# First two expert pairs loaded by single row blocks, softmax and counts moved into the first product, and the last pairs' products in another order

## The chip, the cores and the metric

The kernel runs on one core of one Trainium2 chip. The metric is the time of one execution in device microseconds (us). Three runs of the kernel before took 1381.09, 1384.05 and 1386.32 us, a median of 1384.05.

## The reference, cut to what matters

One encoder layer over 256 tokens of 1024 channels in float32. A mixer (a gated DeltaNet and a gated short convolution) gives `x`, which the change leaves alone. Then come a normalisation, a router and a mixture of experts, in which nearly all of the change lies:

```python
logits = hf @ router_w + router_b                     # 256 tokens, 32 experts
top_val, top_idx = lax.top_k(logits, 4)
gates = softmax(top_val)
# for each expert, on the tokens that chose it:
gate, up = split(h @ w1[e] + b1[e])                   # w1[e]: 1024 x 2048
act = min(gate, 7) * sigmoid(1.702 * gate) * (clip(up, -7, 7) + 1)
y = act @ w2[e] + b2[e]                               # w2[e]: 1024 x 1024
x = x + gt_f * (sum over the 4 experts of gate * y)
return rmsnorm(x, final_norm_w)
```

The weights of one expert are 8 MB (w1) and 4 MB (w2), and all 32 experts are read.

## The kernel before

**Stages.** The mixer takes the first 425 us or so. Its weights come through the SP queue, and the first expert weights are loaded behind them. The rest is the experts.

**Pairs.** The experts are worked on in 16 pairs (`p` = 0 to 15). Two pairs make a quad (`q`), which shares one gathered input `xq` of 256 slots (8 groups of 32, dealt to the quad's four experts by `GROUPS`). Experts are sorted by how many tokens chose them, so the numbers of the experts from pair 2 on are read from `pidx_i` into registers of SP; pairs 0 and 1 are experts 0 to 3.

**A pair.** The first product (`first_product`, `w1_pair`) runs over eight row blocks `k` of w1, 128 rows each. A row block takes 16 matmuls of 128 x 512, which the trace shows as 32 records of line L1325 (`mm`). In front of it stand the biases (`w1_bias`, L120), and behind it the SwiGLU on VectorE and ScalarE (L1382 to L1386). `turn` (`to_ff`, transposes on L1328) turns the result into `aT`. The second product (`Second`, `block(c)`, four blocks of 32 records) multiplies it by w2. `end` scales its two halves (`scaled`, L1436) and hands back two calls of `combine`, which multiply by the gates and add to `x1` (L1429).

**Order.** The products go 0, 1, then second of 0, first of 2, second of 1, and so on: the second product of `p - 1` stands behind the first of `p`. While it runs in an odd `p`, the input of the next quad is gathered (`gather_part`, two `k` per call into one PSUM bank; the even one is evacuated by ScalarE on L1356, the odd one by VectorE on L1354). `mids`, a table by `k`, says what else is done behind a row block. TensorE's instructions of this stage are pinned, so that its order is the order of the program. Other engines' instructions are placed by a scheduler, which may bring them forward unless they are pinned. DMAs are issued by the queues of SP (weights) and ScalarE (small rows).

**Pair 0.** Its input is gathered with slots `P` that VectorE makes from the ranks `rk` (L1302, L1334), which come from a product on TensorE (L1297 to L1299). `route_counts` is traced behind the first product of pair 0: it copies the selection four times (L1500), counts, sorts, does the softmax (L1518 to L1524) and turns ranks and gates. `route_order` (in pair 1) reads its result.

**The ring of weights.** `RING` has nine slots of 2 MB. A slot is either one tile or two halves (the last two). `load_unit` (L982 for a whole slot, L986 for halves) puts two row blocks of one expert into a slot, as 256 rows of w1 or 512 half rows of w2: row `2p` and row `2p + 1` go to partition `p`. A slot is free when both row blocks have been consumed. Nine slots are filled in the mixer (`prefetch`, pinned): row blocks 0 to 5 of both experts of pair 0, and three slots of pair 1. Row blocks 6 and 7 of pair 0, 4 MB, go into working tiles that are not in use yet (L1316: `fw`, `pg`, `pgT`, two `aT`, two `g`, `u`, `th`, two `ysb`, `e4`).

**The end.** In pair 15 the second product of pair 14 stands inside the first product, behind `k` = 2 to 5, with its two combines behind `k` = 6. Then `to_ff` turns half of the result, and `w2_cols` does the second product by columns: 0 to 767 (two parts) and then 768 to 1023, each followed by its combines and by `finish_part` (squares on L1605, weighing with the final norm's weights on L1614). A branch for tokens over an expert's share (L1710) is not taken. Last come the sum of squares (L1778, L1779), the power -1/2 on POOL (`rsqrt`, L88), a scaling and the output.

Of the kernel before, what the change touches and what calls it, by code (L numbers as in the profile page):

```python
# [20 lines left out]
D = 1024  # L21
KT = D // 128
H = 8
NE = 32
# [29 lines left out]
def encoder_block(ctx, tc, x, c, ada_w, ada_b, norm1_w, w_in, conv_qkv_w, a_log, dt_bias, onorm_w,  # L54
# [79 lines left out]
    with ExitStack() as mix:  # L134
# [832 lines left out]
        def unit():  # L967
            tag = RING[unit_n[0] % len(RING)]
            first = unit_n[0] % len(RING) == RING.index(None)
            unit_n[0] += 1  # L970
            if tag:
                return (wk if tag == "hx" else wp_box[0]).tile([128, 4096], FT, name="wst", tag=tag, bufs=1), None
# [3 lines left out]
        def load_unit(src, fine=False, width=2048, hold=lambda i: i):  # L976
            t, halves = unit()
            r = src.shape[1] // 256
            if t is not None:
                halves = [t[:, 2048 * s:2048 * s + 2048] for s in range(2)]  # L980
            if t is not None and not fine:
                hold(nc.sync.dma_start(t, src.rearrange("e (p r) n -> p (e r n)", r=2 * r)))  # L982
            else:
                v = src.rearrange("e (p s r) n -> s p (e r) n", s=2, r=r)
                for s in range(2):
                    hold(nc.sync.dma_start(halves[s][:, 0:width].rearrange("p (r n) -> p r n", r=r), v[s]))  # L986
            return halves

        def w1_unit(p, c, m, regs, hold=lambda i: i):
            src = (moe_w1[0, 2 * p + m:2 * p + m + 1] if p < 2 else moe_w1[0, ds(regs[2 * (p % 2) + m], 1)])  # L990
            halves = load_unit(src[:, 256 * c:256 * c + 256, :], p == 2 * NQ - 1, hold=hold)
            return [[h[:, 512 * i:512 * i + 512] for i in range(4)] for h in halves]
# [3 lines left out]
        def w1_load(p, k, regs):  # L996
            if k % 2 == 0:
                w = pre.pop((p, k // 2), []) if p < 2 else []
                for m in range(len(w), 2):
                    w.append(w1_unit(p, k // 2, m, regs))  # L1000
                held_w[0] = w
            return [h[k % 2] for h in held_w[0]]

        pieces = iter([(0, c, m) for c in range(3) for m in range(2)] + [(1, 0, 0), (1, 0, 1), (1, 1, 0)])
        owed = [0]

        def prefetch(n=1):
            owed[0] += n
            for _, (p, c, m) in zip(range(owed[0] // 4), pieces):
                pre.setdefault((p, c), []).append(w1_unit(p, c, m, None, pin))  # L1010
            owed[0] %= 4
# [298 lines left out]
    for k, m, ts in ((KT - 2, 0, [fw, spare("pg"), spare("pgT")]), (KT - 2, 1, [spare("aT", 1024), spare("aT", 1024)]),  # L1310
                     (KT - 1, 0, [spare("g"), spare("g"), spare("u"), spare("th")]),
                     (KT - 1, 1, [spare("ysb"), spare("ysb"), e4])):
        c, qs = 0, []
        for t in ts:
            n = t.shape[1]
            nc.sync.dma_start(t, moe_w1[0, m, 768 + k % 2:768 + k % 2 + 255:2, c:c + n])  # L1316
            qs += [t[:, o:o + 512] for o in range(0, n, 512)]
            c += n
        pre.setdefault((0, 3), [[], []])[m].append(qs)

# [22 lines left out]
    def gather_part(P, xq, ks):  # L1343
        p = misc()
        for kk, k in enumerate(ks):
            o = p[:, kk * QS:(kk + 1) * QS]
            n = 0
            for t in range(2):
                for hx in (h2h, h2l):
                    mm(o, hx[:, t, 256 * (k // 2) + k % 2:256 * (k // 2) + k % 2 + 255:2], P[:, t],  # L1350
                                  start=n == 0, stop=n == 3, skip_group_check=True)
                    n += 1
            if k % 2:
                V.tensor_scalar(xq[:, k], o, facp[:, k:k + 1], facp[:, 8 + k:9 + k], op0=OP.mult, op1=OP.add)  # L1354
            else:
                A.activation(xq[:, k], o, AF.Identity, scale=facp[:, k:k + 1], bias=facp[:, 8 + k:9 + k])  # L1356
# [56 lines left out]
    def to_ff(gs, aT=None, halves=(0, 1)):  # L1413
        if aT is None:
            aT = work.tile([128, KT, 128], FT, name="aT", tag="aT", bufs=2)
        for half in halves:
# [23 lines left out]
    class Second:  # L1440
# [21 lines left out]
    def w2_cols(p, parts, aT, gt, regs, mids={}):  # L1462
# [5 lines left out]
        for c1 in range(0, 4, nc_):  # L1468
            w = []
            for m in range(2):  # L1470
                src = w2_rows(p, m, regs)[:, 256 * c1:256 * c1 + 256 * nc_, c0:c0 + n]
                if n > 256:
                    w.append(load_unit(src, True, 2 * n))
                else:
                    t, halves = unit()
                    if t is not None:
                        halves = [t[:, 2048 * s:2048 * s + 2048] for s in range(2)]
# [5 lines left out]
            for c in range(nc_):  # L1483
# [7 lines left out]
                for f in mids.get(c1 + c, ()):  # L1491
                    f()
        for y, (o, no) in zip(ys, parts):
            combine([gt[:, pa]], [scaled(y, o, no)], o, no)
# [3 lines left out]
    def route_counts():  # L1498
        for t in range(2):
            pin(V.tensor_copy(sel4[:, t, 1:4], sel4[:, t, 0:1].to_broadcast([128, 3, NE])))  # L1500
        p = misc()
# [15 lines left out]
        for t in range(2):  # L1517
            V.tensor_scalar(nmx[:, t:t + 1], mx[t][:, 0:1], -1.0, None, op0=OP.mult)  # L1518
            A.activation(ex[:, t], lg[:, t, 0:NE], AF.Exp, bias=nmx[:, t:t + 1])
            pin(V.scalar_tensor_tensor(ex[:, t], ex[:, t], 1.0, sel[:, t], op0=OP.mult, op1=OP.mult,  # L1520
                                       accum_out=den[:, t:t + 1]))
        pin(V.reciprocal(den, den))
        for t in range(2):
            pin(V.tensor_scalar(gat[:, t], ex[:, t, None, :].to_broadcast([128, 4, NE]), den[:, t:t + 1], None,  # L1524
                                op0=OP.mult))
        p = misc()
        for t in range(2):
            tr(p[0:NE, t * 128:(t + 1) * 128], rk[:, t], ident)
            tr(p[:, (2 + t) * 128:(3 + t) * 128], gat[:, t].rearrange("p b e -> p (b e)"), ident)
        rT = work.tile([NE, 2, 128], FT, name="rT", tag="ysb", bufs=2)  # L1530
# [66 lines left out]
    ssf = moe.tile([128, 2, len(PARTS)], FT, name="ssf")  # L1597

    def square(t, i, eng="a"):
# [4 lines left out]
        if eng == "a":  # L1604
            A.activation(junk, xv, AF.Square, accum_out=o)  # L1605
        else:
            V.scalar_tensor_tensor(junk, xv, 1.0, xv, op0=OP.mult, op1=OP.mult, accum_out=o)  # L1607

    def finish_part(xf, i, engs="aa"):
        cs = slice(PARTS[i][0], PARTS[i][0] + PARTS[i][1])  # L1610
        for t in range(2):
            square(t, i, engs[t])
        for t in range(2):
            V.tensor_tensor(xf[:, t, cs], x1[:, t, cs], fw[:, cs], op=OP.mult)  # L1614

    def final_row(h):
# [5 lines left out]
        A.copy(fw[:, 512 * h:512 * h + 512], p)  # L1622
# [26 lines left out]
    for p in range(NP):  # L1649
        q, pa = divmod(p, 2)  # L1650
        at = {k: [] for k in range(KT)}
        for i, f in enumerate(sums.pop(p - 2, ())):
            at[i].append(f)
        if p == 1:
# [22 lines left out]
        if p == 0:  # L1677
            turned.extend(route_counts())
# [138 lines left out]
```

## Time and profile before

| what | before |
|---|---|
| median of three runs | 1384.05 us |
| the profiled execution, its own time | 1383.1 us |
| its span, first to last instruction | 1381.4 us |
| TensorE (PE) busy | 1268.9 us, 92% |
| VectorE (DVE), ScalarE (ACT), GpSimd (POOL) busy | 37%, 20%, 11% |
| read from HBM | 486.82 MB |
| granted clock of TensorE, mean | 0.985 |

Times in the trace are microseconds from the start of the span. A busy TensorE is not TensorE at its peak, since matmuls overlap and their ends are modelled. "Idle before" is the time that the engine stood still before an instruction, with what ended it. The granted clock is 1.00 at 2.4 GHz and 0.50 at 1.2 GHz, the two levels. The DMA share is the mean busy share of the core's 16 DMA engines, and can read slightly over 1.

### The profile page before, as it was taken

How to read it: one execution, taken by the hardware profiler on the slowest of the kernel's cores; microseconds unless marked ns; L12 is line 12 of the kernel's file. 1: busy time of each engine (PE TensorE's matmuls, PEld its weight loads, DVE VectorE, ACT ScalarE, POOL GpSimd, SP SyncE). 2: the span in 40 equal slices, each digit the busy share in tenths (PEclk: the TensorE clock that was granted, in tenths of full speed). 3: DMA queues.
4: the chain of work that ended last, by engine and by line, in shares of the span. 5: the costliest groups of instructions: out<-in, count | busy, mean ns of one | idle time of the engine just before them, and what ended most of it. 6: DMA issues, size and time to landing. Idle time of an engine off the chain costs nothing. (4 is left out here: it accounts for less than half of the span.)

```text
span 1381.4 us, 24052 instructions
## 1 busy us (share of the span) xinstructions
PE 1268.9 (92%) x10284; PEld 661.2 (48%) x10285; DVE 514.7 (37%) x1020; ACT 282.0 (20%) x546; POOL 150.9 (11%) x126
## 2 busy tenths in 40 slices
PE   6999997999999899999998998989899898898986
PEld 4988896999996333223333222322322232232222
DVE  3387879876673232123112212221221212211113
ACT  3455552553652010101001000000100000000001
POOL 4555684000000000000000000000000000000000
PEclk9999999999999899999999999999999999999999
DMA  9978977227796799999999999999999999999993
GB/s 337 306 234 275 334 237 233 70 92 261 246 397 247 313 411 387 419 428 425 423 425 427 425 427 425 424 427 426 426 425 426 427 424 426 423 427 423 421 407 128
DMA packets 112882, 492.65 MB, mean 357 GB/s; under 512 B 8703, under 2 KB 64384, under 8 KB 82562
## 3 DMA queue, kind: packets, MB, share of 16 engines
q1 hardware_dynamic: 108528, 485.94, 88.3%
q10 hardware_dynamic: 4241, 5.12, 1.1%
q8 instruction: 82, 1.34, 0.4%
q14 instruction: 31, 0.25, 0.0%
HBM read 486.82 MB, written 4.21 MB: 355 GB/s over the span
## 5 line engine op out<-in xcount | busy, mean ns | idle before, releaser
L1325 PE MATMUL acc<-wst,XT 128*32 128x512 f32 x4088 | 469.8, 599 | 11.8 <-DMA wst<-in_moe_w_dram 11.8
L1325 PEld LDWEIGHTS acc<-wst,XT 128*32 128x32 f32 x4088 | 129.6, 110 | 326.6 <-issue 304.9
L1325 PE MATMUL acc<-wst,aT 128*32 128x512 f32 (+1 forms) x2112 | 250.2, 588 | 37.6 <-DMA wst<-in_moe_w_dram 36.9
L1325 PEld LDWEIGHTS acc<-wst,aT 128*32 128x32 f32 x2112 | 67.6, 111 | 190.9 <-issue 127.7
L314 PE MATMUL mm<-hh,wl 128*128 128x256 f32 (+1 forms) x520 | 149.4, 288 | 2.2 <-POOL wl L264 1.3
L312 PE MATMUL mm<-hh,wh 128*128 128x256 f32 (+1 forms) x520 | 150.2, 289 | 0.3 <-DVE cacc L560 0.3
L313 PE MATMUL mm<-hh,wh 128*128 128x256 f32 (+1 forms) x520 | 149.4, 287 | 0.0
L263 ACT CAST wh<-raw 128x1024 fp32r<-128x1024 f32 (+1 forms) x89 | 91.9, 1039 | 93.6 <-PE mm L313 54.9
L88 POOL TENSOR_TENSOR rs<-ss,half_m 128x2 f32<-128x2 f32 x3 | 2.1, 702 | 941.0 <-DVE ss L1779 883.6
L312 PEld LDWEIGHTS mm<-hh,wh 128*128 128x128 f32 (+1 forms) x520 | 99.5, 191 | 9.7 <-issue 5.5
L314 PEld LDWEIGHTS mm<-hh,wl 128*128 128x128 f32 (+1 forms) x520 | 99.5, 191 | 6.2 <-issue 2.5
L313 PEld LDWEIGHTS mm<-hh,wh 128*128 128x128 f32 (+1 forms) x520 | 99.5, 191 | 0.9 <-issue 0.8
L264 POOL TENSOR_TENSOR wl<-raw,wh 128x1024 fp32r<-128x1024 f32 x36 | 88.0, 2451 | 71.4 <-ACT wh L263 61.8
L1383 ACT ACTIVATE th<-g 128x512 f32<-128x512 f32 x32 | 20.2, 630 | 357.6 <-DVE g L1382 296.2
L1429 DVE TENSOR_TENSOR x<-x,misc 128x512 f32<-128x512 f32 (+1 forms) x66 | 44.2, 671 | 126.1 <-PE misc L1325 126.1
L1382 DVE TENSOR_SCALAR g<-acc 128x512 f32<-128x512 f32 x32 | 22.0, 688 | 180.6 <-PE acc L1325 180.6
L1436 DVE TENSOR_TENSOR ysb<-acc,gtf 128x512 f32<-128x512 f32 (+1 forms) x33 | 22.2, 675 | 172.0 <-PE acc L1325 172.0
L264 DVE TENSOR_TENSOR wl<-raw,wh 128x1024 fp32r<-128x1024 f32 (+1 forms) x53 | 65.7, 1247 | 28.8 <-ACT wh L263 28.6
L1354 DVE TENSOR_SCALAR XT<-misc,fac 128x256 f32<-128x256 f32 x32 | 17.4, 544 | 140.4 <-PE misc L1325 140.4
L1325 PE MATMUL misc<-ysb,pgT 128*128 128x512 f32 (+1 forms) x132 | 63.9, 606 | 1.6 <-DVE ysb L1436 0.9
L1325 PE MATMUL misc<-P,h2h 128*128 128x256 f32 x128 | 40.5, 339 | 20.5 <-ACT XT L1356 18.4
L1325 PEld LDWEIGHTS misc<-P,h2h 128*128 128x128 f32 x128 | 25.1, 196 | 53.1 <-issue 28.3
(387 smaller groups left out, 1378.9 us busy)
## 6 DMA issues: line engine op xcount, KB each, us to landing
wst<-in_moe_w_dram SPq DMA_DIRECT2D x136, 2048.0 KB, 28.6
wst<-in_moe_w_dram SPq DMA_DIRECT2D x100, 1024.0 KB, 28.6
raw<-in_w_in_dram SPq DMA_DIRECT2D x36, 1024.0 KB, 7.5
raw<-in_ada_w_dram SPq DMA_DIRECT2D x24, 1024.0 KB, 8.3
wst<-in_moe_w_dram SPq DMA_DIRECT2D x8, 768.0 KB, 17.7
raw<-in_w_out_sc_dram SPq DMA_DIRECT2D x4, 1024.0 KB, 10.1
raw<-in_w_up_a_dram SPq DMA_DIRECT2D x4, 1024.0 KB, 5.0
raw<-in_w_o_dram SPq DMA_DIRECT2D x4, 1024.0 KB, 9.9
```

The source lines that it names most:

```text
L88: G.tensor_tensor(dst, src, half_m.to_broadcast([128, n]), op=OP.pow)
L263: a = A.copy(wh, src)
L264: b = (V if job.lo == "v" else G).tensor_tensor(wl, src, wh.bitcast(FT), op=OP.subtract)
L312: PE.matmul(ps, wh[:, k, :], ah[:, k, :], start=k == 0, stop=False, skip_group_check=True)
L313: PE.matmul(ps, wh[:, k, :], al[:, k, :], start=False, stop=False, skip_group_check=True)
L314: PE.matmul(ps, wl[:, k, :], ah[:, k, :], start=False, stop=k == KT - 1, skip_group_check=True)
L1325: return held[0](PE.matmul(*a, **kw))
L1354: V.tensor_scalar(xq[:, k], o, facp[:, k:k + 1], facp[:, 8 + k:9 + k], op0=OP.mult, op1=OP.add)
L1382: V.tensor_scalar(g[:n], g_ps[:n], 7.0, None, op0=OP.min)
L1383: A.activation(th[:n], g[:n], AF.Tanh, scale=0.851)
L1429: V.tensor_tensor(xv, xv, p[:, 0:n], op=OP.add)
L1436: V.tensor_tensor(y, ps[:, 0:n], gtf_box[0][:, c0:c0 + n], op=OP.mult)
```

## The change

1. A slot takes one row block of both experts (`load_rows`) in the first and second products of pairs 0 and 1, for row blocks 6 and 7 of pair 15, and in the second product of pair 14. Other loads stay as they were.
2. Nine slots are still filled ahead: row blocks 0 to 6 of pair 0, and 0 and 1 of pair 1. The working tiles hold row block 7 of pair 0 and row block 4 of pair 1.
3. `softmax`, pinned, is traced behind the first two gathers. `route_counts` stands behind row block 6 of pair 0 and the copies of the turned ranks and gates (`turned_gates`) behind row block 7.
4. `gather_part` does the matmuls of both `k`, then evacuates.
5. In pair 15 only blocks 0 and 1 of pair 14's second product stand inside (behind `k` = 4 and 5). Blocks 2 and 3 follow row block 7, then the turn of pair 15 in one piece, one combine, the first two parts of `w2_cols`, the other combine, and then the parts' combines, one of them behind the last part's matmuls.
6. The squares of the last columns come ahead of their weighing. The division by 1024 and the epsilon go into the final weights (times 32) and into a fourth column of the sums.

```diff
-        def unit():
+        def slot():
...
+        def load_rows(srcs, hold=lambda i: i):
+            _, halves = slot()
+            for h, src in zip(halves, srcs):
+                hold(nc.sync.dma_start(h, src))
+            return halves
...
+        def w1_rows(p, k, regs, hold=lambda i: i):
+            c = 256 * (k // 2) + k % 2
+            return [quarters(h) for h in load_rows(
+                [w1_src(p, m, regs)[:, c:c + 255:2].rearrange("e p n -> p (e n)") for m in range(2)], hold)]
...
         def w1_load(p, k, regs):
+            if p < 2 or p == 2 * NQ - 1 and k >= KT - 2:
+                return pre.pop((p, k), None) or w1_rows(p, k, regs)
             if k % 2 == 0:
-                w = pre.pop((p, k // 2), []) if p < 2 else []
-                for m in range(len(w), 2):
-                    w.append(w1_unit(p, k // 2, m, regs))
-                held_w[0] = w
-            return [h[k % 2] for h in held_w[0]]
-
-        pieces = iter([(0, c, m) for c in range(3) for m in range(2)] + [(1, 0, 0), (1, 0, 1), (1, 1, 0)])
+                c = 256 * (k // 2)
+                held_w[0] = [load_unit(w1_src(p, m, regs)[:, c:c + 256]) for m in range(2)]
+            return [quarters(h[k % 2]) for h in held_w[0]]
+
+        pieces = iter([(0, k) for k in range(KT - 1)] + [(1, 0), (1, 1)])
...
-    for k, m, ts in ((KT - 2, 0, [fw, spare("pg"), spare("pgT")]), (KT - 2, 1, [spare("aT", 1024), spare("aT", 1024)]),
-                     (KT - 1, 0, [spare("g"), spare("g"), spare("u"), spare("th")]),
-                     (KT - 1, 1, [spare("ysb"), spare("ysb"), e4])):
+    for p, k, m, ts in ((0, KT - 1, 0, [spare("g"), spare("g"), spare("u"), spare("th")]),
+                        (0, KT - 1, 1, [spare("ysb"), spare("ysb"), spare("pg"), spare("pgT")]),
+                        (1, 4, 0, [spare("aT", 1024), spare("aT", 1024)]), (1, 4, 1, [e4, fw])):
...
                     mm(o, hx[:, t, 256 * (k // 2) + k % 2:256 * (k // 2) + k % 2 + 255:2], P[:, t],
                                   start=n == 0, stop=n == 3, skip_group_check=True)
                     n += 1
+        for kk, k in enumerate(ks):
+            o = p[:, kk * QS:(kk + 1) * QS]
             if k % 2:
...
         def block(self, c):
-            if c % 2 == 0:
-                self.w = [load_unit(w2_rows(self.p, m, self.regs)[:, 256 * c:256 * c + 512], self.p == 2 * NQ - 2)
-                          for m in range(2)]
-            w = [h[c % 2].rearrange("p (i n) -> p i n", i=2) for h in self.w]
+            if self.p < 2 or self.p == 2 * NQ - 2:
+                w = load_rows([w2_rows(self.p, m, self.regs)[:, 512 * (c // 2):512 * (c // 2) + 512]
+                               .rearrange("e (p s r) n -> s p (e r n)", s=2, r=2)[c % 2] for m in range(2)])
+            else:
...
+    def softmax():
         for t in range(2):
             pin(V.tensor_copy(sel4[:, t, 1:4], sel4[:, t, 0:1].to_broadcast([128, 3, NE])))
+        for t in range(2):
+            pin(V.tensor_scalar(nmx[:, t:t + 1], mx[t][:, 0:1], -1.0, None, op0=OP.mult))
+            pin(A.activation(ex[:, t], lg[:, t, 0:NE], AF.Exp, bias=nmx[:, t:t + 1]))
...
     for k in range(2):
         gather_part(P0, xq, (k,))
+    softmax()
     busy(2)
...
+    ssf = moe.tile([128, 2, len(PARTS) + 1], FT, name="ssf")
+    G.memset(ssf[:, :, len(PARTS):], D * EPS)
...
-        A.copy(fw[:, 512 * h:512 * h + 512], p)
+        A.activation(fw[:, 512 * h:512 * h + 512], p, AF.Copy, scale=float(D) ** 0.5)
...
+        if p == 0:
+            at[KT - 2].append(lambda: turned.append(route_counts()))
+            at[KT - 1].append(lambda: turned.extend(turned_gates(turned.pop())))
...
-            at[2].append(lambda: box.append(second(p - 1)))
-            for c in range(4):
-                at[2 + c].append(lambda c=c: box[0].block(c))
-            at[5].append(lambda: box.extend(box[0].end()))
-            at[6] += [lambda h=h: box[1 + h]() for h in range(2)]
+            at[4].append(lambda: box.append(second(p - 1)))
+            for c in range(2):
+                at[4 + c].append(lambda c=c: box[0].block(c))
...
-    last = (to_ff(gs[NP - 1], None, (0,)), gts[NQ - 1], regs[NQ - 1])
-    w2_cols(NP - 1, PARTS[0:2], *last, {0: [lambda: to_ff(gs[NP - 1], last[0], (1,))]})
-    for i in range(2):
-        finish_part(xf, i)
-    w2_cols(NP - 1, PARTS[2:3], *last)
+    for c in range(2, 4):
+        box[0].block(c)
+    turn(NP - 1)
+    before = box[0].end()
+    before[0]()
+    last = (aTs[NP - 1], gts[NQ - 1], regs[NQ - 1])
+    most = w2_cols(NP - 1, PARTS[0:2], *last)
+    before[1]()
+    most[0]()
+    finish_part(xf, 0)
+    rest = w2_cols(NP - 1, PARTS[2:3], *last)
+    most[1]()
+    finish_part(xf, 1)
+    rest[0]()
...
-    finish_part(xf, len(PARTS) - 1, "av")
...
-    V.tensor_reduce(ss3, ssf, axis=mybir.AxisListType.X, op=OP.add)
-    V.tensor_scalar(ss3, ss3, 1.0 / D, EPS, op0=OP.mult, op1=OP.add)
+    square(0, len(PARTS) - 1)
+    square(1, len(PARTS) - 1, "v")
+    pin(V.tensor_reduce(ss3, ssf, axis=mybir.AxisListType.X, op=OP.add))
     rsqrt(rs3, ss3)
+    weigh(xf, len(PARTS) - 1, pin)
```

## Rows read from the trace of the kernel before

**Rows 1.** The page: busy tenths of TensorE and DMA in 40 slices of the span

```profile
PE   6999997999999899999998998989899898898986
...
DMA  9978977227796799999999999999999999999993
```

**Rows 2.** Busy table: stretch, PE, PEld, DVE, ACT, POOL busy, clock, DMA share, GB/s

```profile
439.00:444.00 5.00, 5.00 (x48) 1.75 (x44) 0.54 (x1) 0.28 (x1) 0.00 (x0) 1.00 0.29 63
...
473.00:488.00 15.00, 15.00 (x110) 5.13 (x114) 4.05 (x25) 0.63 (x2) 0.00 (x0) 0.79 0.39 120
...
540.00:548.00 8.00, 8.00 (x55) 2.35 (x57) 2.75 (x4) 0.00 (x0) 0.00 (x0) 1.00 0.75 265
548.00:1200.00 652.00, 601.74 (x4822) 193.80 (x4818) 139.82 (x298) 42.69 (x73) 0.00 (x0) 0.99 1.01 425
...
1338.00:1360.00 22.00, 20.22 (x170) 7.06 (x166) 8.88 (x14) 2.46 (x4) 0.00 (x0) 1.00 0.83 309
```

**Rows 3.** Timeline of SP's queue, 434 to 600: start, duration, line, loads issued

```profile
442.28 17.82 SPq L982 DMA_DIRECT2D wst<-in_moe_w_dram  x6
...
544.66 28.63 SPq L982 DMA_DIRECT2D wst<-in_moe_w_dram  x7
```

**Rows 4.** Timeline of VectorE, 426 to 436: start, duration, line, operation, idle before

```profile
430.75 0.19 DVE L1520 SCALAR_TENSOR_TENSOR ex<-ex,sel 128x32 f32<-128x32 f32 x1 [1.45 <-ACT ex L1519]
...
431.79 0.22 DVE L1302 SCALAR_TENSOR_TENSOR rk<-misc,sel 128x64 f32<-128x64 f32 x1
```

**Rows 5.** Timeline of TensorE, 415 to 600 (same columns)

```profile
429.18 0.39 PE L1299 MATMUL misc<-sel,tri_s 128*128 128x32 f32 x2
...
432.69 0.36 PE L1325 MATMUL misc<-P,h2h 128*128 128x256 f32 x1 [2.15 <-DVE P L1334]
...
462.06 4.89 PE L1325 MATMUL acc<-wst,XT 128*32 128x512 f32 x42
471.45 1.06 PE L1325 MATMUL misc<-sel,one_f 128*128 128x32 f32 x4 [4.50 <-DVE sel L1500]
...
474.12 2.09 PE L120 MATMUL acc<-b1c,tri_ul 32*128 32x512 f32 x8
476.14 8.62 PE L1325 MATMUL acc<-wst,XT 128*32 128x512 f32 x64
...
496.92 7.07 PE L1325 MATMUL acc<-wst,XT 128*32 128x512 f32 x64
...
513.46 0.28 PE L1325 MATMUL misc<-P,h2l 128*128 128x256 f32 x1
514.40 0.39 PE L1325 MATMUL misc<-P,h2h 128*128 128x256 f32 x1 [0.66 <-ACT XT L1356]
```

**Rows 6.** DMA totals of 450 to 470 (2 MB loads), then 1290 to 1300 (1 MB loads)

```profile
DMA packets 588, 8.59 MB, mean 429 GB/s; under 512 B 64, under 2 KB 64, under 8 KB 64
...
DMA packets 578, 4.21 MB, mean 421 GB/s; under 512 B 64, under 2 KB 64, under 8 KB 64
```

**Rows 7.** Timeline of TensorE, 1262 to 1376

```profile
1282.60 1.24 PE L1328 MATMUL misc<-ident,g 128*128 128x128 f32 x8
...
1326.51 4.52 PE L1325 MATMUL acc<-wst,aT 128*32 128x512 f32 x25 [4.02 <-DMA wst<-in_moe_w_dram]
...
1341.68 3.89 PE L1325 MATMUL misc<-ysb,pgT 128*128 128x512 f32 x8
...
1355.07 7.95 PE L1325 MATMUL acc<-wst,aT 128*32 128x512 f32 x96
...
1367.26 3.66 PE L1325 MATMUL acc<-wst,aT 128*32 128x256 f32 x64
```

**Rows 8.** Timeline of VectorE, 1370 to 1377

```profile
1372.20 0.85 DVE L1429 TENSOR_TENSOR x<-x,misc 128x256 f32<-128x256 f32 x2 [0.79 <-PE misc L1325]
...
1374.47 0.15 DVE L1778 TENSOR_REDUCE ss<-ssf 128x2 f32<-128x6 f32 x1
1374.65 0.17 DVE L1779 TENSOR_SCALAR ss<-ss 128x2 f32<-128x2 f32 x1
```

More of the change, by code (lines that the diff above doesn't have):

```diff
@@ L971, in unit, with load_unit @@
             if tag:
-                return (wk if tag == "hx" else wp_box[0]).tile([128, 4096], FT, name="wst", tag=tag, bufs=1), None
+                t = (wk if tag == "hx" else wp_box[0]).tile([128, 4096], FT, name="wst", tag=tag, bufs=1)
+                return t, [t[:, 2048 * s:2048 * s + 2048] for s in range(2)]
             return None, [wp_box[0].tile([128, 2048], FT, name="wst", tag="s8", bufs=1) if first and s == 0 else
                           raw_tile([128, 2048], FT, "wst") for s in range(2)]
-        def load_unit(src, fine=False, width=2048, hold=lambda i: i):
-            t, halves = unit()
+        def load_unit(src, width=2048, fine=False):
+            t, halves = slot()
             r = src.shape[1] // 256
-            if t is not None:
-                halves = [t[:, 2048 * s:2048 * s + 2048] for s in range(2)]
             if t is not None and not fine:
-                hold(nc.sync.dma_start(t, src.rearrange("e (p r) n -> p (e r n)", r=2 * r)))
+                nc.sync.dma_start(t, src.rearrange("e (p r) n -> p (e r n)", r=2 * r))
             else:
@@ L1008, in prefetch @@
             owed[0] += n
-            for _, (p, c, m) in zip(range(owed[0] // 4), pieces):
-                pre.setdefault((p, c), []).append(w1_unit(p, c, m, None, pin))
+            for _, (p, k) in zip(range(owed[0] // 4), pieces):
+                pre[p, k] = w1_rows(p, k, None, pin)
             owed[0] %= 4
@@ L1309, in encoder_block @@
     e4 = dp.tile([128, 1024], FT, name="wst", tag="e4")
-    for k, m, ts in ((KT - 2, 0, [fw, spare("pg"), spare("pgT")]), (KT - 2, 1, [spare("aT", 1024), spare("aT", 1024)]),
-                     (KT - 1, 0, [spare("g"), spare("g"), spare("u"), spare("th")]),
-                     (KT - 1, 1, [spare("ysb"), spare("ysb"), e4])):
-        c, qs = 0, []
+    for p, k, m, ts in ((0, KT - 1, 0, [spare("g"), spare("g"), spare("u"), spare("th")]),
+                        (0, KT - 1, 1, [spare("ysb"), spare("ysb"), spare("pg"), spare("pgT")]),
+                        (1, 4, 0, [spare("aT", 1024), spare("aT", 1024)]), (1, 4, 1, [e4, fw])):
+        o, qs = 0, []
+        c = 256 * (k // 2) + k % 2
         for t in ts:
             n = t.shape[1]
[L1316 to L1319, printed above, removed]
+            nc.sync.dma_start(t, moe_w1[0, 2 * p + m, c:c + 255:2, o:o + n])
+            qs += [t[:, i:i + 512] for i in range(0, n, 512)]
+            o += n
+        pre.setdefault((p, k), []).append(qs)
     held = [pin]
@@ L1411, in w1_pair, with to_ff @@
         return [swiglu(128, pss[half], pss[2 + half]) for half in range(2)]
[L1413 to L1416, printed above, removed]
+    def to_ff(gs):
+        aT = work.tile([128, KT, 128], FT, name="aT", tag="aT", bufs=2)
+        for half in range(2):
             ps = misc()
@@ L1472, in w2_cols @@
                 if n > 256:
-                    w.append(load_unit(src, True, 2 * n))
+                    w.append(load_unit(src, 2 * n, True))
                 else:
-                    t, halves = unit()
-                    if t is not None:
-                        halves = [t[:, 2048 * s:2048 * s + 2048] for s in range(2)]
+                    _, halves = slot()
                     for h in range(2):
@@ L1490, in w2_cols, with route_counts @@
                                           tile_position=(0, 32 * j), skip_group_check=True)
[L1491 to L1494, printed above, removed]
+        return [lambda o=o, no=no, y=scaled(y, o, no): combine([gt[:, pa]], [y], o, no) for y, (o, no) in zip(ys, parts)]
     gtf_box = []
-    def route_counts():
+    def softmax():
         for t in range(2):
             pin(V.tensor_copy(sel4[:, t, 1:4], sel4[:, t, 0:1].to_broadcast([128, 3, NE])))
+        for t in range(2):
+            pin(V.tensor_scalar(nmx[:, t:t + 1], mx[t][:, 0:1], -1.0, None, op0=OP.mult))
+            pin(A.activation(ex[:, t], lg[:, t, 0:NE], AF.Exp, bias=nmx[:, t:t + 1]))
+        for t in range(2):
+            pin(V.scalar_tensor_tensor(ex[:, t], ex[:, t], 1.0, sel[:, t], op0=OP.mult, op1=OP.mult,
+                                       accum_out=den[:, t:t + 1]))
+        pin(V.reciprocal(den, den))
+        for t in range(2):
+            pin(V.tensor_scalar(gat[:, t], ex[:, t, None, :].to_broadcast([128, 4, NE]), den[:, t:t + 1], None,
+                                op0=OP.mult))
+    def route_counts():
         p = misc()
@@ L1516, in route_counts @@
         V.tensor_scalar(perm, tgt.rearrange("p q m -> p (q m)"), key[:, 1:2], None, op0=OP.is_equal)
[L1517 to L1525, printed above, removed]
         p = misc()
@@ L1529, in route_counts, with turned_gates @@
             tr(p[:, (2 + t) * 128:(3 + t) * 128], gat[:, t].rearrange("p b e -> p (b e)"), ident)
+        return p
+    def turned_gates(p):
         rT = work.tile([NE, 2, 128], FT, name="rT", tag="ysb", bufs=2)
```

29 lines of the change are left out of this document (16 added, 13 removed).

## The prediction

> **What bounds the kernel now.** I read the page's slices first. From about the fourteenth slice on, DMA and TensorE both read 9 or nearly so [rows 1], so the page alone does not say which one sets the pace. The busy table of chosen stretches does: from 548 to 1200 us the DMA share is 1.01 at 425 GB/s [rows 2]. DMA never rests there, while TensorE has 50 of 652 us idle. The second half is therefore bound by the weights' bytes, and a microsecond that DMA loses earlier comes out at the end.
>
> The same table shows where it loses time. At 425 GB/s the stretch 439 to 444 (63 GB/s) lost 5 x (1 - 63/425) = 4.3 us, 473 to 488 lost 10.8 us and 540 to 548 lost 3.0 us: 18.1 us together [rows 2]. The queue that issues the loads says why. Six loads start at 442.28 and seven at 544.66 [rows 3], each right after a pair of row blocks has been consumed: DMA had nothing to load into. TensorE sets those moments, so up to 548 TensorE is the bound, and after it DMA.
>
> Third comes TensorE's own order in that stretch [rows 4, 5]. It waits 4.50 us for the selection copies at 471.45, between the first products of pairs 0 and 1, and afterwards 64 records of row blocks take 8.62 us where a later 64 take 7.07 [rows 5]: the granted clock of 473 to 488 is 0.79 [rows 2].
>
> **Part 1: softmax behind the slots.** VectorE runs the softmax (from 430.75) ahead of the ranks at 431.79, from which P is made [rows 4]. The ranks' TensorE operand ended at 429.18 + 0.39 = 429.57 [rows 5]. With the softmax traced and pinned behind the gather, ranks and P move up by 431.79 - 429.63 (a handover of 0.06 by estimate) = 2.1 us, and pair 0 with them. The softmax itself, under 2 us of VectorE and ScalarE, then lies beside row blocks during which VectorE is nearly idle (0.54 of the 5 us from 439 [rows 2]); without that cover it would cost those 2 us again, and the second gather's evacuation queues behind it at worst.
>
> **Part 2: counts inside pair 0.** Now TensorE ends pair 0 at 462.06 + 4.89 = 466.95, idles, does counts and turns from 471.45, biases, then two row blocks that end at 476.14 + 8.62 = 484.76 [rows 5]. After the change the sequence is 466.95, plus counts and turns (471.45 to 474.12, or 2.67 at the lower clock, so 1.3 at the upper, by estimate), plus biases 1.1 (half of 2.09 and a handover), plus two row blocks 7.1: 476.5. That is 8.3 us earlier. VectorE's count chain and ScalarE's two copies are now queued ahead of the SwiGLU of pair 0, and the third and fourth bias of pair 1 wait for two of its reads; the row block of 3.5 us covers them. Uncovered, the bound is the old 4.5 us wait with its clock loss, so this term lies between 0 and 8.3.
>
> **Part 3: gather evacuated after both halves.** In pair 1's second product the second four gather matmuls start at 514.40, 0.94 us after the fourth began (513.46), where neighbours follow at 0.12 [rows 5]. Writing both halves of the bank before reading either saves 0.8 us, four times: 3.3 us. In later pairs it saves as much, but there TensorE has slack and it buys nothing.
>
> Together TensorE reaches the end of pair 2's second row block 2.1 + 8.3 + 3.3 = **13.7 us** earlier.
>
> **Part 4: single row blocks in the ring.** A 2 MB slot now holds one row block of both experts and is free after one row block, where two slots came free after two. At 425 GB/s a slot takes 4.9 us. Walk DMA on: the spares' loads end near 439.4; row 0 has freed a slot at 436, so the 439 hole goes. Seven slots come free inside pair 0 (six before), and keep DMA busy to 439.4 + 9 x 4.9 = 483.5 once pair 1's first two rows free theirs at 473 and 476.5; so the 473 hole goes. Eighteen slots in all last to 528. The next one waits for pair 2's second row block, in the old run 544.66 and now 544.66 - 13.7 = 531. A hole of 3 us stays, and DMA runs on without rest from there, 13.7 us ahead. So DMA's own bound is 18.1, TensorE's 13.7, and **the smaller counts**. After that, which slot holds what is as before. The queue issues two loads for one, at 0.3 to 0.4 us each against 4.9 us per slot, so that costs nothing unless issue takes over 2.4 us.
>
> Size of a load: 2 MB loads stream at 429 GB/s, 1 MB loads at 421 [rows 6]. Thirteen slots of row loads, 27.3 MB, come after 439 us; on these that is 1.2 us, inside the hole that stays. I take 0; the far end is the 309 GB/s of the slowest loads [rows 2], among the rivals.
>
> The Trainium skill, "DMA: Bandwidth & Descriptors" (Bandwidth, Measured), speaks against smaller loads: it gives 341 GB/s for one of 1 MB and 425 for 16 MB. By that, an estimate, the 27.3 MB would cost 16 us more and the end would come near 1375. The trace disagrees: with loads queued behind one another, 421 [rows 6].
>
> **Part 5: the tail.** Before, TensorE waited last for weights at 1326.51 [rows 7]; five more 1 MB blocks of these experts land by 1326.5 + 5 x 2.46 = 1338.8. Then it still had row blocks, two combines (3.89), row block 7 at 1345.50, an exposed SwiGLU, and the last second product, whose last add ended at 1373.05 [rows 7, 8].
>
> New order, on the same scale: the last landing is pair 14's fourth block, 1338.8. It takes 3.5, half of 7.07 (1342.3), pair 15's turn 1.2, one combine 1.9 (1345.4), two blocks of the last product at 7.95/3 = 2.65 each (1350.7) [rows 5, 7]. SwiGLU lies beside pair 14's blocks. The third block needs the seventh of eight loads of 256 x 768 floats, 0.79 MB each: at 309/0.83 = 372 GB/s [rows 2] 14 us or so after 1338.8, so 1352.8, a wait of 2.1. Two blocks to 1358.1, two combines 3.8 (1361.9), the last 64 records 3.66 (1365.6), then as now 2.1 to the last add: 1367.7. Gain 1373.05 - 1367.7 = **5.3 us**. With no wait it would be 7.4. If the waits for single blocks (some 1.5 us each at pair 14's third and fourth) bring the lower clock, it is 0 or less. I take 5.3: TensorE's wait of 2.15 us at 432.69 [rows 5] is nearest to these, and the clock of 439 to 444 still reads 1.00 [rows 2].
>
> **Part 6: the last columns.** The two weighings leave the path to the power (they fit beside POOL's 0.7) and one scaling of 0.17 goes: the reduce at 1374.47 can start at 1373.9, and L1779 with its handover is 0.18 [rows 8]. Gain 0.7. The final weights' scale by 32 is free, being in a copy.
>
> **Sum.** 13.7 + 5.3 + 0.7 = 19.7, off the profiled execution's 1383.1 (span 1381.4 and 1.7 around it): 1363.4. The median of the runs, 1384.05, is 1 us above that execution. I round to **1364**.
>
> **Rivals.**
> *The tail gives nothing* (0.12): waits for single blocks take back what the order saves, or the lower clock returns. For it: three new waits on loads; against it: row block 7's weights land two slots, 9.8 us, ahead of pair 14's last block, so the SwiGLU has cover. 1383.1 - 13.7 - 0.7 = 1368.7.
> *The hole between pairs 0 and 1 stays* (0.10): the bias of pair 1 waits on SwiGLU behind the count chain on VectorE, and the lower clock returns. 13.7 - 8.3 = 5.4; with the tail, 1383.1 - 5.4 - 6.0 = 1371.7.
> *Row loads stream slower* (0.04): every second 8 KB row is read. At the 309 GB/s of the slowest weight loads seen [rows 2], DMA loses 27.3/0.309 - 27.3/0.425 = 24 us where it gains 18.1, and the end is 1383.1 + 6 - 6.0 = 1383. The 421 of the 1 MB loads [rows 6], which read every second row too, speaks against it. This is the rule of the Trainium skill's page named above, carried to this kernel.
> *TensorE falls to the lower clock over pair 1* (0.05), the one that ends slower: row-wise hand-over makes it pause before each row, and its clock stays at 1.2 GHz. A row block costs 3.5 us more there; over the eight rows of pair 1 that is 28 us against 13.7, so 1383.1 + 14.3 - 6.0 = 1391. It decides from (13.7 + 6.0)/3.5 = 6 slow row blocks on. Against it: the loads of pair 1 have landed 20 us before use.
> *It does not do what it says* (0.04): the scheduler already hoisted softmax once; if it places counts late again and DMA order is unchanged, about 1381.
>
> **Numbers.** The forecast has 0.65. Its own bounds run from 1383.1 - 18.1 - 7.4 - 0.7 = 1357 to some 1367. The range 1358 to 1374 takes in the first two rivals and leaves out the last three, and the forecast's far end. Half a per cent, 7 us, is about what a measurement of this kernel can tell from no change: faster 0.87 (the forecast and the first two rivals), same 0.08 (the third and the last), slower 0.05.
>
> **What would show it.** Right: ranks near 429.6 and pair 0's first row block near 432.3; no 4.5 us wait before the counts, and clock 1.00 from 460 to 500; DMA share near 1 from 430 to 528 with one short hole near 530; no wait for the gather's evacuation; the last weights' wait of TensorE inside the last product, and SwiGLU of pair 15 beside pair 14's blocks. Wrong: a hole near 470, a rate under 410 GB/s between 440 and 530, new holes after 535, or TensorE idle over 5 us in all after the last row block of pair 15.

## The result, and the profile after

The changed kernel takes 1366.03 us (median; 1365.88 to 1366.79), the kernel before 1384.88 in the same measurement. The ratio is 0.987, with a 95% interval of 0.985 to 0.989. The forecast was 1364 us, with a range of 1358 to 1374. The profiled execution of after took 1366.79 us with a span of 1364.9. The span is 16.5 us under that of before, and this is the difference taken apart here. Only line numbers are new: `mm` is L1337, `load_rows` L992, `load_unit` L981 (whole slots) and L985 (halves).

**The holes of DMA.** The busy table of after, with the columns of [rows 2]: stretch, PE, PEld, DVE, ACT and POOL busy, clock, DMA share, GB/s.

```profile
439.00:444.00 5.00, 5.00 (x48) 1.75 (x44) 0.55 (x1) 0.00 (x0) 0.00 (x0) 1.00 1.02 425
473.00:488.00 15.00, 15.00 (x140) 5.21 (x136) 5.34 (x28) 0.79 (x2) 0.10 (x1) 1.00 1.03 427
525.00:535.00 10.00, 10.00 (x68) 2.97 (x64) 2.76 (x4) 0.00 (x0) 0.00 (x0) 1.00 0.65 247
...
548.00:1200.00 652.00, 603.02 (x4798) 197.32 (x4791) 145.15 (x306) 43.07 (x74) 0.00 (x0) 0.98 1.01 425
```

The two holes that read 63 and 120 GB/s before are gone (425 and 427), and TensorE's clock in the second is 1.00 instead of 0.79. The hole of 540 to 548 is now at 525 to 535, where DMA loses 10 x (1 - 247/425) = 4.2 us. SP's queue has eight loads to issue there, and takes 21 us for them, since it waits for TensorE to free slots:

```profile
520.35 21.02 SPq L992 DMA_DIRECT2D wst<-in_moe_w_dram  x8
```

**TensorE up to pair 2.** First VectorE's ranks, then the timeline of TensorE (start, duration, line, operation, count, idle before). These answer to [rows 4, 5].

```profile
430.17 0.22 DVE L1314 SCALAR_TENSOR_TENSOR rk<-misc,sel 128x64 f32<-128x64 f32 x1 [0.33 <-PE misc L1311]
```

```profile
429.74 0.39 PE L1311 MATMUL misc<-sel,tri_s 128*128 128x32 f32 x2
...
461.83 0.63 PE L1337 MATMUL misc<-sel,one_f 128*128 128x32 f32 x4
...
466.84 1.14 PE L120 MATMUL acc<-b1c,tri_ul 32*128 32x512 f32 x8
467.92 7.07 PE L1337 MATMUL acc<-wst,XT 128*32 128x512 f32 x64
...
516.00 0.75 PE L1340 MATMUL misc<-ident,g 128*128 128x128 f32 x4 [0.69 <-ACT aT L1433]
...
531.53 1.98 PE L1337 MATMUL misc<-ysb,pgT 128*128 128x512 f32 x4
```

The ranks now wait only for their own operand from TensorE. The counts (461.83) show no wait, the two row blocks behind the bias take 7.07 instead of 8.62, and pair 2's second row block ends at 531.53, where the next instruction starts. In before that instruction was:

```profile
544.55 1.98 PE L1325 MATMUL misc<-ysb,pgT 128*128 128x512 f32 x4
```

One small wait is new: a turn waits 0.69 us for ScalarE, once in this stretch (in before the same turn waited 0.21 us for VectorE). What the counts waited for before are VectorE's copies of the selection. First in before, then in after:

```profile
471.15 0.40 DVE L1500 COPY sel<-sel 128x96 f32<-128x96 f32 x2
```

```profile
434.00 0.40 DVE L1513 COPY sel<-sel 128x96 f32<-128x96 f32 x2
```

**The tail.** TensorE from 1320 us on; this answers to [rows 7].

```profile
1320.91 3.64 PE L1337 MATMUL acc<-wst,aT 128*32 128x512 f32 x32 [0.51 <-DMA wst<-in_moe_w_dram]
1325.87 3.62 PE L1337 MATMUL acc<-wst,aT 128*32 128x512 f32 x26 [1.33 <-DMA wst<-in_moe_w_dram]
...
1332.78 6.21 PE L1337 MATMUL acc<-wst,aT 128*32 128x512 f32 x68
1339.32 5.35 PE L1337 MATMUL acc<-wst,aT 128*32 128x512 f32 x60 [0.33 <-DMA wst<-in_moe_w_dram]
1344.60 4.22 PE L1337 MATMUL misc<-ysb,pgT 128*128 128x512 f32 x8
1348.75 3.66 PE L1337 MATMUL acc<-wst,aT 128*32 128x256 f32 x64
```

The waits for weights are short, 0.33 to 1.33 us, and there are three. The last 64 records end at 1348.75 + 3.66 = 1352.41; before they ended at 1370.92 [rows 7]. That is 18.5 us, of which the front (pair 2's second row block, 544.55 in the timeline of before to 531.53) makes 13.0 and the new tail 5.5.

**The output store.** VectorE's last instructions in after and the first output, then SP's wait for the output (total, times, longest).

```profile
1354.52 0.75 DVE L1442 TENSOR_TENSOR x<-x,misc 128x256 f32<-128x256 f32 x2
...
1357.18 0.88 DVE L1817 TENSOR_SCALAR XT<-XT,rs 128x512 f32<-128x512 f32 x2 [0.25 <-POOL rs L88]
...
1357.70 0.84 SPq L1818 DMA_DIRECT2D out_dram<-XT  x2
```

```profile
SPq L1846 <- DMA out_dram<-XT: 5.1, 2, 4.5
```

The same scaling and the same wait in before, two views:

```profile
1375.70 0.88 DVE L1783 TENSOR_SCALAR XT<-XT,rs 128x512 f32<-128x512 f32 x2 [0.88 <-POOL rs L88]
```

```profile
SPq L1812 <- DMA out_dram<-XT: 2.9, 4, 1.1
```

From the scaling to the end of the span it is 1364.9 - 1357.18 = 7.7 us in after and 1381.4 - 1375.70 = 5.7 in before: 2.0 us are given back behind every instruction of the change. The view of DMA of after, from 1358 to the end, lists what shares that time with the store (queue, kind, packets, MB, share), and the busy table shows the store's pace:

```profile
q1 hardware_dynamic: 288, 0.52, 20.6%
...
q8 instruction: 1, 0.02, 1.4%
```

```profile
1360.00:1361.00 1.00, 0.00 (x0) 0.00 (x0) 0.00 (x0) 0.00 (x0) 0.00 (x0) 0.50 1.01 367
1361.00:1362.00 1.00, 0.00 (x0) 0.00 (x0) 0.00 (x0) 0.00 (x0) 0.00 (x0) 0.50 0.36 137
1362.00:1363.00 1.00, 0.00 (x0) 0.00 (x0) 0.00 (x0) 0.00 (x0) 0.00 (x0) 0.50 0.07 27
```

An instruction fetch, one packet of 0.02 MB, falls into the store; its share, 1.4% of sixteen engines over 7 us, is some 1.6 us of one engine. The bulk is through within 1361 to 1362; then the share is 0.07, about one engine of sixteen, at 27 GB/s. In before the same view lists that queue between 1374 and 1377 and not between 1377 and the end.

So the 16.5 us are 13.0 of the front, 5.5 of the tail, -0.7 between the last matmul and the last add, +0.7 from the last add to the scaling, and -2.0 in the store.

### The profile page after: what moved, and what is told of

It is laid out like the page before. It is cut to its first block, busy times and chain, and to the rows that moved or that the text cites. A ratio compares the mean times of both kernels' runs of the same rounds, so it can differ in the third digit from the quotient of the medians.

```text
span 1364.9 us, 24037 instructions
## 1 busy us (share of the span) xinstructions
PE 1267.2 (93%) x10284; PEld 663.1 (49%) x10285; DVE 514.7 (38%) x1019; ACT 281.9 (21%) x546; POOL 150.3 (11%) x127
## 5 line engine op out<-in xcount | busy, mean ns | idle before, releaser
L1337 PE MATMUL acc<-wst,XT 128*32 128x512 f32 x4088 | 472.5, 596 | 15.0 <-DMA wst<-in_moe_w_dram 14.9
L1337 PE MATMUL acc<-wst,aT 128*32 128x512 f32 (+1 forms) x2112 | 259.3, 604 | 40.7 <-DMA wst<-in_moe_w_dram 40.6
L1337 PEld LDWEIGHTS acc<-wst,XT 128*32 128x32 f32 x4088 | 133.8, 110 | 328.6 <-issue 293.9
L1337 PEld LDWEIGHTS acc<-wst,aT 128*32 128x32 f32 x2112 | 69.8, 113 | 199.5 <-issue 131.9
L1337 PE MATMUL misc<-ysb,pgT 128*128 128x512 f32 (+1 forms) x132 | 63.9, 606 | 0.3 <-ACT aT L1433 0.2
L560 DVE SCALAR_TENSOR_TENSOR cacc<-mm,col,cacc 128x254 f32<-128x254 f32 (+1 forms) x96 | 46.1, 480 | 9.0 <-ACT cacc L557 6.9
L1370 ACT ACTIVATE XT<-misc,fac 128x256 f32<-128x256 f32 x32 | 18.1, 566 | 141.8 <-PE misc L1337 141.8
```

What stands on the lines that cost most here:

```text
L560: V.scalar_tensor_tensor(a[:, o0:o1], p[:, s0:s1], cw(j), a[:, o0:o1], op0=OP.mult, op1=OP.add)
L1337: return held[0](PE.matmul(*a, **kw))
```

## The experiments

Each run undoes or changes one part of the changed kernel, e7 two. The kernel before stood beside each at 1384.96 us (e1 to e4) and 1385.35 us (e5 to e8). The changed kernel was not timed again beside them, and before's median moved by up to 0.5 us between the three measurements, so a difference to after is uncertain by about as much.

**e1: the ring as before.** Pairs 0 and 1 in slots of two row blocks of one expert; the working tiles hold row blocks 6 and 7 of pair 0. TensorE's order and the tail stay.

```diff
...
-            if p < 2 or p == 2 * NQ - 1 and k >= KT - 2:
-                return pre.pop((p, k), None) or w1_rows(p, k, regs)
+            if p < 2:
+                if k % 2 == 0:
+                    w = pre.pop((p, k // 2), [])
+                    for m in range(len(w), 2):
+                        w.append(w1_unit(p, k // 2, m, regs))
+                    held_w[0] = w
+                return [h[k % 2] for h in held_w[0]]
...
-            if self.p < 2 or self.p == 2 * NQ - 2:
+            if self.p == 2 * NQ - 2:
```

> The changed kernel with the ring of pairs 0 and 1 as before (two row blocks of one expert in a slot, row blocks 6 and 7 of pair 0 in the working tiles). Theory: TensorE sets the pace up to pair 2's second row block, so the ring is worth only what DMA then still lacks. Holes come back near 440 and 471 to 475, the hole near 530 goes, and the twelve slots loaded from about 474.3 on last to 533.5 where the changed kernel goes on at 532.4: 1 to 2.5 us longer, 1367 to 1368.5. Rival: the row-wise ring is what brought the gain of the first part; then most of its 13 us is lost and the time is near 1379.

Measured: 1367.56 us (1366.66 to 1367.96), 1.5 over after. The busy table of e1:

```profile
437.00:444.00 7.00, 7.00 (x65) 2.40 (x68) 0.54 (x1) 0.57 (x1) 0.00 (x0) 1.00 0.71 239
465.00:480.00 15.00, 15.00 (x140) 4.98 (x136) 9.28 (x33) 1.63 (x3) 0.00 (x0) 1.00 0.93 358
525.00:535.00 10.00, 10.00 (x68) 2.97 (x64) 2.75 (x4) 0.00 (x0) 0.00 (x0) 1.00 1.03 423
```

The first two holes are back, but small: 7 x (1 - 239/425) = 3.1 and 15 x (1 - 358/425) = 2.4 us. The third is filled in return. DMA loses 5.4 us where after loses 4.2. The new ring brought 1.5 us of 19 by the medians, 1.2 by the scaling of the output (1358.41 here, 1357.18 in after).

**e2: the counts behind pair 0 again,** with the softmax and the selection copies still early.

```diff
-        if p == 0:
-            at[KT - 2].append(lambda: turned.append(route_counts()))
-            at[KT - 1].append(lambda: turned.extend(turned_gates(turned.pop())))
...
         first_product(p, at)
+        if p == 0:
+            turned.extend(turned_gates(route_counts()))
```

> The changed kernel with the counts and the turned gates behind the first product of pair 0 as before, the softmax with its selection copies still early. Theory: the 4.50 us wait was for the selection copies queued behind the SwiGLU on VectorE, so with these early the place of the counts hardly matters: 0 to 1 us longer, and no fall of the clock near 470. Rival, the prediction's own wording (the counts have to lie inside the product): the wait and the lower clock come back, 8 us longer, 1374.

Measured: 1365.88 us (1365.47 to 1366.28), as after. TensorE of e2:

```profile
465.56 0.63 PE L1337 MATMUL misc<-sel,one_f 128*128 128x32 f32 x4
...
468.08 7.07 PE L1337 MATMUL acc<-wst,XT 128*32 128x512 f32 x64
```

No wait, and the two row blocks start 0.16 us later than in after. Where the counts stand is not what matters; that their operands are early is, as e7 below shows.

**e3: the gather's evacuations as before,** each behind its own half of the bank.

```diff
                     n += 1
-        for kk, k in enumerate(ks):
-            o = p[:, kk * QS:(kk + 1) * QS]
             if k % 2:
```

> The changed kernel with each half of the gather evacuated before the second half is written, as before. Theory: TensorE is the bound up to pair 2's second row block, so four waits of 0.8 us come out at the end: 3.2 us longer, 1369.2, and the hole near 530 grows by as much. Rival: TensorE has slack there, 0 us.

Measured: 1370.07 us (1369.54 to 1371.84), 4.0 over after where 3.2 was expected; its span is 2.9 longer. Not all of it is the gather's: the operand of the ranks comes at 430.96 in e3 and at 429.74 in after, so 1.2 us are lost in the mixer, and why is open. The end of pair 2's second row block in e3, then DMA's last hole, which has grown (busy table):

```profile
536.00 1.98 PE L1337 MATMUL misc<-ysb,pgT 128*128 128x512 f32 x4
```

```profile
525.00:540.00 15.00, 14.82 (x104) 4.78 (x108) 4.59 (x13) 0.13 (x1) 0.00 (x0) 1.00 0.59 230
```

The row block ends 536.00 - 531.53 = 4.5 us later, 3.3 without the mixer's 1.2. The hole is 15 x (1 - 230/425) = 6.9 us against 4.2: most of what TensorE loses ahead of pair 2, DMA loses in the hole and the run at its end.

**e4: the tail as before,** with the changed rings for pairs 0 and 1 and the short end. The order of the products of pairs 14 and 15 and their loads by single row blocks are undone together, so the run does not tell the two apart.

```diff
...
-            at[4].append(lambda: box.append(second(p - 1)))
-            for c in range(2):
-                at[4 + c].append(lambda c=c: box[0].block(c))
+            at[2].append(lambda: box.append(second(p - 1)))
+            for c in range(4):
+                at[2 + c].append(lambda c=c: box[0].block(c))
+            at[5].append(lambda: box.extend(box[0].end()))
+            at[6] += [lambda h=h: box[1 + h]() for h in range(2)]
...
+    last = (to_ff(gs[NP - 1], None, (0,)), gts[NQ - 1], regs[NQ - 1])
+    for f in w2_cols(NP - 1, PARTS[0:2], *last, {0: [lambda: to_ff(gs[NP - 1], last[0], (1,))]}):
+        f()
```

> The changed kernel with pairs 14 and 15 in the order of before (pair 14's second product and combines inside the first product of 15, the turn of 15 in halves), the last columns' squares as changed. Theory: 4.8 us longer, 1370.8, since TensorE again ends 34 us after the last weights of pair 14 and 15's row blocks instead of some 29.5. Rival: the order of the tail gives nothing, the same time.

Measured: 1371.11 us (1370.66 to 1372.04), 5.1 over after. Its tail shows the old pattern: one long wait, then row block 7 (1332.77) and an exposed SwiGLU, for which the turn at 1337.51 waits. The last 64 records end at 1354.54 + 3.66 = 1358.20, 5.8 us later than in after.

```profile
1313.40 4.89 PE L1337 MATMUL acc<-wst,aT 128*32 128x512 f32 x25 [3.89 <-DMA wst<-in_moe_w_dram]
...
1332.77 3.64 PE L1337 MATMUL acc<-wst,XT 128*32 128x512 f32 x32
1337.51 0.75 PE L1340 MATMUL misc<-ident,g 128*128 128x128 f32 x4 [1.09 <-DVE g L1400]
1338.95 2.79 PE L1337 MATMUL acc<-wst,aT 128*32 128x512 f32 x32 [0.69 <-ACT aT L1434]
```

**e5: the last columns as before** (weighing, scale and epsilon ahead of the power).

```diff
...
-    pin(V.tensor_reduce(ss3, ssf, axis=mybir.AxisListType.X, op=OP.add))
-    rsqrt(rs3, ss3)
-    weigh(xf, len(PARTS) - 1, pin)
+    weigh(xf, len(PARTS) - 1, lambda i: i)
+    V.tensor_reduce(ss3, ssf, axis=mybir.AxisListType.X, op=OP.add)
+    V.tensor_scalar(ss3, ss3, 1.0 / D, EPS, op0=OP.mult, op1=OP.add)
+    rsqrt(rs3, ss3)
```

> Part 6 alone undone: the weighings, the scale by 1/1024 and the add of the small constant stand ahead of the power again. Theory (the last columns save 0.74 us, but the finished output then meets a 16 KB instruction fetch on one DMA engine that had ended just before the stores in the kernel before): scaling starts 0.7 us later than in the changed kernel, the fetch ends at or before the first store, the stores' last byte comes at most 0.3 us later or up to 1.3 us earlier; the run 1364.7 to 1366.3 us against 1366.0 for the changed kernel. Rival (the fetch has nothing to do with it, the time from scaling to the end is what it is): the run is 0.7 us longer, 1366.7.

Measured: 1365.92 us (1365.56 to 1366.9), 0.1 under after: part 6 is worth nothing here. The scaling starts 0.8 us later and the end comes only 0.3 later (1365.2). VectorE and SP's wait in e5:

```profile
1357.96 0.88 DVE L1817 TENSOR_SCALAR XT<-XT,rs 128x512 f32<-128x512 f32 x2 [0.88 <-POOL rs L88]
```

```profile
SPq L1846 <- DMA out_dram<-XT: 4.6, 2, 4.0
```

The fetch still overlaps the store here (the longest wait is 4.0 us, 4.5 in after), so this run alone weakens the rival's 1366.7 but does not settle the cause. The next does.

**e8: no branch.** The conditional part for tokens over an expert's share is left out; with this input it never runs.

```diff
-    with tc.If(n_over > 0):
...
-        for i in range(len(PARTS) - 1):
-            finish_part(xf, i)
```

> Leaves out the conditional part that handles experts with more tokens than their places (with this input it never runs). Theory (the branch causes the late instruction fetch that falls into the output stores): no 16 KB fetch during the stores, from scaling to the end of the span 5.7 us as in the kernel before or less instead of 7.7, and the run some 2 us shorter, 1364 us; somewhat more if the branch itself cost the engines time. Rival (the stores are slower for another reason): the time from scaling to the end stays at 7.7 us and the run at 1366.

Measured: 1364.59 us (1364.0 to 1364.73), 1.4 under after. The scaling, SP's wait, the queues from 1357 to the end, and the store by the busy table, all of e8:

```profile
1356.67 0.88 DVE L1752 TENSOR_SCALAR XT<-XT,rs 128x512 f32<-128x512 f32 x2 [0.25 <-POOL rs L88]
```

```profile
SPq L1781 <- DMA out_dram<-XT: 3.2, 2, 2.6
```

```profile
q1 hardware_dynamic: 288, 0.52, 25.4%
q10 hardware_dynamic: 288, 0.52, 24.9%
```

```profile
1360.00:1361.00 1.00, 0.00 (x0) 0.00 (x0) 0.00 (x0) 0.00 (x0) 0.00 (x0) 0.50 0.84 313
1361.00:1362.00 1.00, 0.00 (x0) 0.00 (x0) 0.00 (x0) 0.00 (x0) 0.00 (x0) 0.50 0.00 0
```

No fetch is listed, and the store stops at once instead of dribbling on. From the scaling to the end it is 1362.6 - 1356.67 = 5.9 us, 1.8 less than in after. The scaling comes another 0.5 earlier; 0.2 of it lie between the last add and the scaling, where the branch stood (1354.98 to 1356.67 here, 1355.27 to 1357.18 in after), and 0.3 ahead of the branch. The fetch belongs to the branch, and the slow end to the fetch. Of the 2.3 us by which the span is shorter, the median shows 1.4; the profiled execution of after is the slowest of its four. The store also differs among the other runs: from the scaling to the end it is 6.5 us in e3, 6.8 in e4 and e7, and 7.9 in e1. So spans tell a part's worth less well than the scaling does, which comes 4.1 us later than in after in e3, 5.2 in e4 and 11.1 in e7.

**e7: softmax and counts as before,** parts 1 and 2 of the prediction undone together.

```diff
...
-    softmax()
     busy(2)
...
-        if p == 0:
-            at[KT - 2].append(lambda: turned.append(route_counts()))
-            at[KT - 1].append(lambda: turned.extend(turned_gates(turned.pop())))
...
+        if p == 0:
+            turned.extend(turned_gates(route_counts()))
```

> Softmax and counts as in the kernel before: softmax ahead of the ranks by the scheduler's choice, selection copies and counts behind the first product of pair 0. The rest of the changed kernel stays. Theory (TensorE sets the place of the last hole of DMA, so what TensorE loses up to pair 2 comes out at the end): ranks 2.2 us later, TensorE waits again some 4.5 us for the selection copies and then has the lower clock, 8 to 10 us later at pair 2's second row block, and the run is 8 to 10 us longer, 1374 to 1376 us. Rival (the ring by single row blocks alone brings the gain, TensorE's order there does not matter): 1366 to 1368.

Measured: 1376.85 us (1376.71 to 1378.73), 10.8 over after, a little past the range expected. The timeline of TensorE and then the busy table, of e7:

```profile
473.48 0.63 PE L1337 MATMUL misc<-sel,one_f 128*128 128x32 f32 x4 [4.50 <-DVE sel L1513]
```

```profile
440.00:445.00 5.00, 5.00 (x48) 2.10 (x48) 0.00 (x0) 0.57 (x1) 0.00 (x0) 1.00 0.81 298
475.00:490.00 15.00, 15.00 (x112) 4.79 (x114) 4.36 (x27) 0.62 (x2) 0.00 (x0) 0.80 0.56 216
535.00:545.00 10.00, 10.00 (x68) 2.97 (x64) 2.18 (x4) 0.00 (x0) 0.00 (x0) 1.00 0.53 198
```

The wait of 4.50 us for the copies is back to the hundredth, and so is the wait of 2.15 us for P behind the softmax (at 433.49); with them come the clock of 0.80 and holes of 1.5, 7.4 and 5.3 us: 14.2 in all, 10.0 more than after's 4.2. With e2 this gives the whole effect to the early copies and softmax.

**e6: pair 2 by single row blocks too.**

```diff
-            if p < 2 or p == 2 * NQ - 1 and k >= KT - 2:
+            if p < 3 or p == 2 * NQ - 1 and k >= KT - 2:
```

> Pair 2's first products are also loaded by single row blocks, so that its first row block frees a slot 3.5 us or more before its second. Theory (the hole of 4.2 us that DMA still has near 530 is only the wait for pair 2's second row block, and every microsecond of it comes out at the end): the hole shrinks to under 1 us and the run is 3 to 4 us shorter, some 1362.5 us. Rival 1 (the hole moves to the next place where two slots come free together, some 5 us later): 0 to 1 us, 1365 to 1366. Rival 2 (smaller loads are slower): longer than 1366.

Measured: 1364.11 us (1362.99 to 1364.55), ratio 0.985 (0.984 to 0.986), 1.9 under after, and no run of one lies among those of the other. It is the fastest version that computes everything. The hole is gone (busy table of e6):

```profile
525.00:535.00 10.00, 10.00 (x68) 2.96 (x64) 2.75 (x4) 0.00 (x0) 0.00 (x0) 1.00 1.01 419
535.00:550.00 15.00, 14.07 (x120) 3.99 (x112) 0.00 (x0) 0.60 (x1) 0.00 (x0) 1.00 1.03 428
```

The theory held for the hole, not for the size: 4.2 us were filled, the span is 2.4 shorter. The rest is gone well before the tail: TensorE's waits for weights end 2.2 us earlier than in after already near 777 (776.80 against 779.03), 2.3 at 1298.71 and still 2.3 at 1323.58 (after: 1325.87). First after's timeline, then that of e6:

```profile
1301.00 3.19 PE L1337 MATMUL acc<-wst,aT 128*32 128x512 f32 x25 [1.34 <-DMA wst<-in_moe_w_dram]
```

```profile
1298.71 4.89 PE L1337 MATMUL acc<-wst,aT 128*32 128x512 f32 x25 [1.32 <-DMA wst<-in_moe_w_dram]
...
1323.58 3.62 PE L1337 MATMUL acc<-wst,aT 128*32 128x512 f32 x26 [1.32 <-DMA wst<-in_moe_w_dram]
```

The 25 records at 1298.71 take 4.89 us where after's take 3.19, and that cost nothing by 1323.58. Some of the missing 4.2 - 2.3 = 1.9 us goes earlier: from 440 to 520, where neither run has a hole, DMA reads 421 GB/s in e6, which loads pair 2 by single row blocks there, and 424 in after, 80 x (1 - 421/424) = 0.6 us. The rest is open.

## Why the prediction was right, and where not

**Part 1** (2.1): ranks 431.79 to 430.17, 1.6 us. Their operand itself came 0.56 later (429.18 to 429.74), so 2.2 by the step's own working. That shift, in the mixer, is most of what the front lacks to 13.7; what made it is open.

**Part 2** (8.3): the row blocks end at 474.99 instead of 484.76, 9.8 us; less part 1's 1.6 it is 8.15. The size was right and the label was not: "counts inside pair 0" was named as the step, and e2 shows that their place is worth nothing. The copies that TensorE waited for stand in the new `softmax`, far ahead; e7 undoes that and loses 10.8 us, where parts 1 and 2 were costed at 10.4. That the size came out is in part luck: the step took the wait as gone because the counts moved, and it went because the same edit moved the copies.

**Part 3** (3.3): the fifth gather matmul now starts 0.12 us behind the fourth, where it was 0.94. e3 gives back 4.0, and 3.3 at pair 2's second row block once the mixer's 1.2 are taken off: the size of the step. The 0.69 us wait for ScalarE behind the third gather was not foreseen.

**Part 4** ("the smaller counts", 13.7 with a hole of 3 us near 530): 13.0, and 4.2 us at 525 to 535. The mechanism held in e3 and e7: microseconds of TensorE before pair 2 become microseconds of DMA's hole and of the end. In e6 only about half of the hole did. What the step left out is what the ring is worth by itself: 1.2 to 1.5 us by e1, because an earlier TensorE frees old slots earlier too. Row loads stream as forecast: 421 GB/s from 450 to 470, where the 2 MB loads of before read 429, and TensorE sets the pace there, so that it does not show in the time. The figure of the Trainium skill, "DMA: Bandwidth & Descriptors" (Bandwidth, Measured), of 341 GB/s for a load of 1 MB, which the page gives for loads issued from GpSimd, does not carry to the loads of SP that queue behind one another here.

**Part 5** (5.3): 5.5 at the last matmul, 4.8 at the last add; by e4 5.8 at the last matmul and 5.1 in the time. The wait of 2.1 us at the third block was 0.33, while the four blocks and two combines up to the last part took 15.6 us without it, 1.2 more than the 14.4 of the step. The wait itself was worked out loosely: seven loads of 0.79 MB at 372 GB/s are 14.8 us, not 14, and in after the third block's weights come 1339.32 - 1325.87 = 13.45 us behind pair 14's fourth block. Two adds and weighings of the middle part now stand ahead of the last ones on VectorE, 2.86 us instead of 2.13 from the last matmul to the last add; the step said "as now".

**Part 6** (0.7): the scaling comes 0.74 closer to the last add, as worked out, and the run gains nothing (e5). The sum ended at the scaling and took the store as a constant. It was not: the fetch that ended before the store now falls into it, 2.0 us. This is the term that was missing; with it 1363.4 becomes 1365.4, against 1366.79 of the profiled execution. The other 1.4 are 0.7 of the front, 0.5 of the tail up to the last add, and 0.2 by which the execution exceeds its span more than in before (1.9 against 1.7).

**Rivals.** That the tail gives nothing falls with e4. That the hole between pairs 0 and 1 stays is what e7 looks like, and only because copies and softmax were put back. Row loads at 309 GB/s did not come: they stream at 421 from 450 to 470. The clock over pair 1 reads 1.00, so the slower case did not come near. The last, that nothing moves, falls with the copies at 434.00.

## What to carry to other kernels

Where a stall waits for an operand, ask which instruction makes the operand early, not where the consumer stands; e2 and e7 split the two, and only one was worth anything. A ring with finer slots pays only for the holes that are left once the engine that frees slots is on time, and one more pair in it (e6, 1.9 us) was then worth about as much as the first two (e1, 1.5 us). Behind the last instruction the store of the output is a stage with other traffic of its own: look at its queue list before counting microseconds saved ahead of it.

## What was unexpected of the hardware

By the trace a fetch of instructions goes through the same DMA engines as data and shows as a queue of its own ("q8 instruction", one packet of 0.02 MB). Where it fell into the 1 MB store, the store ended with a share of 0.07, about one engine of sixteen, at 27 GB/s, and 2.0 us later. It came with a branch that is not taken: without the branch the fetch is not there, and SP's longest wait for the store is 2.6 us instead of 4.5.
